# FFN1's first product with the tokens stationary, its gate on token-major tiles, and transposes behind it

## The chip, the cores and the metric

The kernel runs on one core of one Trainium2 chip. The metric is the device time of one execution in microseconds (us); the number given for a kernel is the median of its timed runs. A profiled execution has a trace beside its time: the span runs from the first to the last instruction in it. Engines are called PE (TensorE; PEld is its weight load), DVE (VectorE), ACT (ScalarE), POOL (GpSimd) and SP (the queue that issues most transfers).

## The reference, cut to what matters

256 tokens of width 2048 go through two blocks. The change lies in the feed-forward part of the first one:

```python
D_MODEL, SEQ, D_FF = 2048, 256, 5632

def _rmsnorm(x, g, eps=1e-6):
    return x * lax.rsqrt(jnp.mean(x * x, axis=-1, keepdims=True) + eps) * g

def first_block(x, ...):
    ...                                   # mixer: attention, recurrence, w_out
    x = x + _rmsnorm(mix, g_mix_post)
    h = _rmsnorm(x, g_ffn_pre)            # (256, 2048)
    gu = h @ w_ffn_in                     # (2048, 2 * 5632): gate columns, then up columns
    f = silu(gu[..., :D_FF]) * gu[..., D_FF:]
    x = x + _rmsnorm(f @ w_ffn_out, g_ffn_post)
    return x
```

All values are float32.

## The kernel before, in words

Every large product multiplies in the `fp32r` form, with each operand split into a high and a low part; three of the four products of parts are summed. Weights come in tiles `W` of 512 KB (128 partitions x 1024 floats). For each, `split` (L157 to L163) issues the load on SP, lets ACT write the high part `WH` (L162) and DVE the low part `WL` (L163). There are three buffers each of `WH` and `WL` and four of `W`. The activations lie in `HL` tiles, high and low part side by side. One such weight tile with its products is the unit of this document: FFN1's first product has 176 of them, its second one (`w_ffo`) 88. SP issues the loads in program order.

There are two forms of the product.

- `gemm_t` (L182) keeps the weights stationary: a 128 x 128 piece of `WH` is loaded into PE and the tokens' high and low parts stream past it together (512 columns, L210), then a piece of `WL` with the high part alone (256 columns, L209 or L212). One weight tile is 8 such pairs, 16 matmuls. The result has features on the partitions and tokens along the free axis, with the two halves of the sum next to each other, so that an evacuation has to add them. With `lead=4` the first four tiles are gone through once for each half of the tokens, in matmuls of 256 and 128 columns.
- `gemm_steps` (L107) keeps the tokens stationary: a 128 x 128 piece of `HL` is loaded and 512 columns of `WH` or `WL` stream past it, three matmuls (L145, L146, L147) for each of 2 token halves and 2 slices of depth, 12 matmuls for one weight tile. The result has tokens on the partitions and is already the whole sum. With `lead=4` it goes through the first four tiles for the first token half, then for the second.

`ffn1` (L1131) runs in three parts of 8, 8 and 6 feature blocks of 256. For each block the gate product and the up product are made (4 weight tiles each), and then, for each of the two 128-feature halves of a block, this follows: ACT copies one half of the sum (L1145), DVE adds the other (L1146); for the gate DVE multiplies by `R` (L1152), ACT takes the silu (L1154) and POOL multiplies by `R` again (L1155); for the up part DVE multiplies by the gate (L1161), ACT writes the high part of f (L1163) and POOL the low one (L1164). `R` is 1/rms of the tokens laid along the free axis; `spread` (L1118) makes it with two matmuls once `rms` (L1105) has summed the squares. After each part the second product with `w_ffo` runs in the `gemm_steps` form over that part's features.

Beside FFN1 a table for the second block is made on POOL: `s5_table` (L1565) computes eight groups by doubling (L1586) and sends each to memory from POOL's own queue (L1590). Its tile `R` has two buffers, so a new group's first write (L1578) waits for the transfer of the group before the last. Each of these chores is a Python generator in a lane; a product calls `tick` twice per weight tile, which advances each lane.

Before FFN1, `w_out` ends with the residual sum and norm: `pn_x` (L1072) adds into `xr`, `pn_tr` (L1082) transposes `xr` on PE (L64, 4 transposes of 128 x 128 into one PSUM tile), and ACT (L1100) and DVE (L1101) write the high and low part of each 128-feature slice, scaled by `g_ffn_pre`. `halves_t` (L1409) orders these pieces for `gemm_t`: all four of token half 0 first. `halves` (L1390) orders them for `gemm_steps`. The step from FFN1 to the second block's first product (`w_in_2`, L1195 to L1199) already uses `halves` and `gemm_steps` with a lead.

## Time and profile before

| | before |
|---|---|
| median of 3 runs | 3405.7 us (3399.62 to 3407.25) |
| the profiled execution's own time | 3411.74 us |
| its span | 3409.9 us |
| PE busy | 3291.0 us (97%) |
| PEld busy | 2743.1 us (80%) |
| DVE busy | 2258.8 us (66%) |
| ACT busy | 1697.8 us (50%) |
| POOL busy | 790.3 us (23%) |
| granted PE clock, mean | 0.983 of full speed |
| `w_ffi` loads, issue to landing | 176 of 512 KB, 3.9 us |

The shares are means over the whole span; a stage has its own. A granted clock of 1.00 is 2.4 GHz and one of 0.50 is 1.2 GHz.

### The profile page before, as it was taken

How to read it: one execution, taken by the hardware profiler on the slowest of the kernel's cores; microseconds unless marked ns; L12 is line 12 of the kernel's file. 1: busy time of each engine (PE TensorE's matmuls, PEld its weight loads, DVE VectorE, ACT ScalarE, POOL GpSimd, SP SyncE). 2: the span in 40 equal slices, each digit the busy share in tenths (PEclk: the TensorE clock that was granted, in tenths of full speed). 3: DMA queues.
4: the chain of work that ended last, by engine and by line, in shares of the span. 5: the costliest groups of instructions: out<-in, count | busy, mean ns of one | idle time of the engine just before them, and what ended most of it. 6: DMA issues, size and time to landing. Idle time of an engine off the chain costs nothing.

```text
span 3409.9 us, 50346 instructions
## 1 busy us (share of the span) xinstructions
PE 3291.0 (97%) x18954; PEld 2743.1 (80%) x18954; DVE 2258.8 (66%) x3505; ACT 1697.8 (50%) x2641; POOL 790.3 (23%) x970
## 2 busy tenths in 40 slices
PE   8999999999999999999999999899999999999998
PEld 7887777877888888888888887677677888888886
DVE  5776786855666766654555557966777775666576
ACT  5545455444555445444443444365555554454453
POOL 0203122422111204880210212720121321111021
PEclk9999999999999999999999999999999999999999
DMA  6453543556656774556566566445356456656664
GB/s 214 155 181 101 162 131 123 177 160 210 196 177 210 245 251 145 191 191 194 187 188 193 186 196 227 145 160 191 116 193 200 145 185 192 188 186 192 191 186 154
DMA packets 180485, 615.19 MB, mean 180 GB/s; under 512 B 23099, under 2 KB 28300, under 8 KB 179472
## 3 DMA queue, kind: packets, MB, share of 16 engines
q1 hardware_dynamic: 169088, 580.01, 53.5%
q0 software_dynamic: 10288, 30.33, 2.7%
q8 instruction: 149, 2.44, 0.3%
q10 hardware_dynamic: 864, 1.62, 0.1%
q14 instruction: 96, 0.79, 0.1%
HBM read 588.36 MB, written 26.66 MB: 180 GB/s over the span
## 4 chain that ended last, share of the span: by engine, by line
PE 68%; DVE 8%; issue 8%; POOL 5%; DMA 4%; ACT 2%; DVEq 0%; POOLq 0%; ACTq 0%; SPq 0%
PE pm L210 22%; PE pm L209 10%; PE pm L145 9%; PE pm L146 9%; PE pm L147 9%; DVE WL L163 3%; PE ps L64 1%; POOL s5ro L1586 1%; POOL s5rt L1586 1%; DMA pd<-s5rt 1%; ACT WH L162 1%; DMA T<-dT 1%; PE pm L212 1%; PE ps L1879 0%; DMA dT<-TM 0%
## 5 line engine op out<-in xcount | busy, mean ns | idle before, releaser
L163 DVE TENSOR_TENSOR WL<-W,WH 128x1024 fp32r<-128x1024 f32 (+2 forms) x1016 | 1283.3, 1264 | 828.5 <-ACT WH L162 822.8
L210 PE MATMUL pm<-HL,WH 128*128 128x512 f32 x4928 | 1749.8, 401 | 8.7 <-ACT WH L162 4.4
L162 ACT ACTIVATE WH<-W 128x1024 fp32r<-128x1024 f32 (+2 forms) x1016 | 1066.3, 1050 | 1047.0 <-PE pm L210 442.0
L209 PE MATMUL pm<-HL,WL 128*128 128x256 f32 x4620 | 1315.8, 285 | 17.7 <-DVE WL L163 16.2
L210 PEld LDWEIGHTS pm<-HL,WH 128*128 128x128 f32 x4928 | 916.1, 190 | 213.2 <-DVE pt L495 7.0
L209 PEld LDWEIGHTS pm<-HL,WL 128*128 128x128 f32 x4620 | 878.5, 190 | 42.4 <-DVE WL L163 20.8
L145 PE MATMUL pm<-WH,HL 128*128 128x512 f32 (+1 forms) x1472 | 586.1, 399 | 1.1 <-ACT WH L162 1.1
L146 PE MATMUL pm<-WL,HL 128*128 128x512 f32 (+1 forms) x1472 | 577.8, 393 | 6.7 <-DVE WL L163 6.7
L147 PE MATMUL pm<-WH,HL 128*128 128x512 f32 (+1 forms) x1472 | 575.8, 391 | 0.7 <-DVE HL L1096 0.7
L146 PEld LDWEIGHTS pm<-WL,HL 128*128 128x128 f32 x1472 | 278.1, 189 | 65.3 <-DVE WL L163 9.7
L145 PEld LDWEIGHTS pm<-WH,HL 128*128 128x128 f32 x1472 | 277.5, 189 | 62.2 <-issue 4.1
L147 PEld LDWEIGHTS pm<-WH,HL 128*128 128x128 f32 x1472 | 277.9, 189 | 58.4 <-DVE HL L1096 1.1
L2147 POOL TENSOR_TENSOR fcv<-fcv,fcv 128x256 f32<-128x256 f32 x44 | 51.5, 1170 | 544.6 <-DVE fcv L2134 440.1
L1155 POOL TENSOR_TENSOR sg<-sg,spr 128x256 f32<-128x256 f32 x44 | 43.2, 999 | 303.3 <-ACT sg L1154 303.3
L212 PE MATMUL pm<-HL,WL 128*128 128x256 f32 x308 | 87.3, 283 | 1.4 <-DVE WL L163 1.4
L1164 POOL TENSOR_TENSOR HL<-fu,HL 128x256 fp32r<-128x256 f32 x44 | 49.5, 1143 | 128.5 <-ACT HL L1163 128.5
L2133 DVE SCALAR_TENSOR_TENSOR fcv<-fu,cw,fcv 128x255 f32<-128x255 f32 x88 | 54.3, 617 | 32.4 <-ACT fcv L2132 32.4
L1586 POOL TENSOR_TENSOR s5ro<-s5rt,s5un 128x8 f32<-128x8 f32 (+7 forms) x128 | 73.0, 584 | 4.9
L2132 ACT ACTIVATE fcv<-fu,cw 128x256 f32<-128x256 f32 x88 | 52.5, 596 | 40.5 <-DVE fu L2131 40.5
L212 PEld LDWEIGHTS pm<-HL,WL 128*128 128x128 f32 x308 | 58.6, 190 | 14.8 <-DVE WL L163 2.7
L1145 ACT ACTIVATE fu<-pm 128x256 f32<-128x256 f32 x88 | 33.8, 384 | 64.3 <-PE pm L210 64.3
L1586 POOL TENSOR_TENSOR s5rt<-s5ro,s5ro 128x4 f32<-128x4 f32 (+7 forms) x128 | 64.4, 524 | 4.9
(519 smaller groups left out, 3291.5 us busy)
## 6 DMA issues: line engine op xcount, KB each, us to landing
W<-in_w_ffi SPq DMA_DIRECT2D x176, 512.0 KB, 3.9
W<-in_w_up SPq DMA_DIRECT2D x176, 512.0 KB, 3.6
W<-in_w_rkv SPq DMA_DIRECT2D x96, 512.0 KB, 3.5
W<-in_w_qkv SPq DMA_DIRECT2D x96, 512.0 KB, 3.6
W<-in_w_ffo SPq DMA_DIRECT2D x88, 512.0 KB, 3.9
W<-in_w_down SPq DMA_DIRECT2D x88, 512.0 KB, 3.6
W<-in_w_gate SPq DMA_DIRECT2D x64, 512.0 KB, 3.8
W<-in_w_out SPq DMA_DIRECT2D x64, 512.0 KB, 4.2
```

The lines of the kernel that those rows point to most:

```text
L145: nc.tensor.matmul(o, a, WH[:, j], start=(k == 0), stop=False)
L146: nc.tensor.matmul(o, a, WL[:, j], start=False, stop=False)
L147: self.mm = nc.tensor.matmul(o, b, WH[:, j], start=False, stop=(k == kts - 1))
L162: self.nc.scalar.activation(WH, W, AF.Copy)
L163: self.gated(self.nc.vector.tensor_tensor(WL, W, WH.bitcast(F32), op=ALU.subtract))
L209: nc.tensor.matmul(o[:, 0, ts], WL[:, kk, c], x[:, 0, ts], start=False, stop=False)
L210: self.mm = nc.tensor.matmul(o[:, :, ts], WH[:, kk, c], x[:, :, ts], start=(k == 0), stop=(k == 15))
L212: nc.tensor.matmul(o[:, 0, ts], WL[:, kk, c], x[:, 0, ts], start=False, stop=False)
L1586: i = nc.gpsimd.tensor_tensor(o, x, y, op=op)
L2132: nc.scalar.activation(c, u, AF.Identity, scale=cw[:, 2, ct:ct + 1], bias=cw[:, 3, ct:ct + 1])
L2133: nc.vector.scalar_tensor_tensor(c[:, 1:], u[:, 0:255], cw[:, 1, ct:ct + 1], c[:, 1:], op0=ALU.mult, op1=ALU.add)
L2147: nc.gpsimd.tensor_tensor(c, c, gs[i], op=ALU.mult)
```

## The change

FFN1's first product goes from `gemm_t` to `gemm_steps`, in 11 feature blocks of 512 with 8 weight tiles for the gate and 8 for the up part. The packing of `w_ffi` changes with it; the number and size of the loads stay. The gate is now one ACT instruction for each token half, the silu of the PSUM tile with 1/rms as its scale (in the changed file L1145). The up part is one DVE instruction for each half that multiplies by 1/rms and by the gate (L1149). Then a generator in lane 4, `turn`, transposes the 128 x 512 tile `sg` in four pieces for each half (L64), and ACT and DVE write the high (L1159) and low part (L1160) of f from PSUM. Line numbers behind L1180 fall by 5: the table's lines are L1572 to L1585. The second product is as it was. In front of FFN1 `halves(..., 4)` takes the place of `halves_t`.

```diff
-                self.halves_t(lambda h, q: self.pn_tr(acc, h2[:, :, 0], h2[:, :, 1], "g_ffn_pre", h, q))
+                self.halves(lambda h, q: self.pn_tr(acc, h2[:, :, 0], h2[:, :, 1], "g_ffn_pre", h, q), 4)
...
-            for bi, b in enumerate(range(2 * blocks[0], 2 * blocks[-1] + 2)):
-                gs = []
-
-                def total(P):
-                    u = fp.tile([128, T], F32, tag="fu", bufs=4, name=self.nm("fu"))
-                    nc.scalar.activation(u, P[:, T:], AF.Copy)
-                    nc.vector.tensor_tensor(u, P[:, :T], u, op=ALU.add)
-                    return u
-
-                def ev_g(nb, P):
-                    for i in range(2):
-                        u = total(P[i])
-                        nc.vector.tensor_tensor(u, u, R, op=ALU.mult)
-                        g = fp.tile([128, T], F32, tag="sg", bufs=4, name=self.nm("sg"))
-                        nc.scalar.activation(g, u, AF.Silu)
-                        nc.gpsimd.tensor_tensor(g, g, R, op=ALU.mult)
-                        gs.append(g)
-
-                def ev_u(nb, P):
-                    for i in range(2):
-                        u = total(P[i])
-                        nc.vector.tensor_tensor(u, u, gs[i], op=ALU.mult)
-                        kk = 2 * bi + i
-                        nc.scalar.activation(fH[:, kk], u, AF.Copy)
-                        nc.gpsimd.tensor_tensor(fL[:, kk], u, fH[:, kk].bitcast(F32), op=ALU.subtract)
+            for bi, b in enumerate(blocks):
+                g = fp.tile([128, 2, 512], F32, tag="sg", bufs=2, name=self.nm("sg"))
+
+                def ev_g(nb, P, g=g):
+                    for h in range(2):
+                        nc.scalar.activation(g[:, h], P[h], AF.Silu, scale=r1[:, h:h + 1])
+
+                def ev_u(nb, P, g=g, bi=bi, fH=fH, fL=fL):
+                    for h in range(2):
+                        nc.vector.scalar_tensor_tensor(g[:, h], P[h], r1[:, h:h + 1], g[:, h], op0=ALU.mult, op1=ALU.mult)
+
+                    def turn():
+                        yield 2
+                        for h in range(2):
+                            ps = self.pst()
+                            for u in range(4):
+                                self.T(ps[:, u * 128:u * 128 + 128], g[:, h, u * 128:u * 128 + 128])
+                            pv = ps.rearrange("p (a b) -> p a b", a=4)
+                            hi, lo = (t[:, 4 * bi:4 * bi + 4, h * 128:h * 128 + 128] for t in (fH, fL))
+                            nc.scalar.activation(hi, pv, AF.Copy)
+                            nc.vector.tensor_tensor(lo, pv, hi.bitcast(F32), op=ALU.subtract)
+                            yield
+                    self.spawn(4, turn())
                 if first:
                     P0 = []
-                    for _ in self.gemm_t(self.i["w_ffi"], [b], xa, lambda nb, P: P0.append(P), lead=4, pre=self.pre):
-                        self.tick()
+                    self.gemm(self.i["w_ffi"], [b], NKT, lambda k: xa(k)[:, 0], lambda k: xa(k)[:, 1], lambda nb, P: P0.append(P), lead=4, pre=self.pre)
                     self.drain(0)
                     r1 = self.rms(fp, xr)
                     self.tap("x1", xr)
                 else:
-                    for _ in self.gemm_t(self.i["w_ffi"], [b], xa, ev_g):
-                        self.tick()
-                for n, _ in enumerate(self.gemm_t(self.i["w_ffi"], [22 + b], xa, ev_u)):
+                    self.gemm(self.i["w_ffi"], [b], NKT, lambda k: xa(k)[:, 0], lambda k: xa(k)[:, 1], ev_g)
+                for n, _ in enumerate(self.gemm_steps(self.i["w_ffi"], [11 + b], NKT, lambda k: xa(k)[:, 0], lambda k: xa(k)[:, 1], ev_u)):
                     self.tick()
                     if first and n == 4:
-                        R = self.spread(fp, r1)
                         ev_g(None, P0[0])
                         first = False
...
-    a["w_ffi"], a["w_ffo"] = _pk_t(f["w_ffn_in"][0]), _pk(f["w_ffn_out"][0])
+    a["w_ffi"], a["w_ffo"] = _pk(f["w_ffn_in"][0]), _pk(f["w_ffn_out"][0])
```

Where the instructions stand is read from the built programs. On POOL, in the first part of FFN1, this stands before; `sg` is the gate after the silu, `spr` is `R`, and `s5rt` and `s5ro` are the table's tiles:

```order
L1586 TENSOR_TENSOR s5ro_13019<-s5rt_12987,s5un 128x4x2
L1578 MEMSET s5rt_13245 128x2
L1586 TENSOR_TENSOR s5ro_13018<-s5rt_12987,s5un 128x4x2
...
L1586 TENSOR_TENSOR s5ro_13091<-s5rt_12987,s5un 128x4x8
L1155 TENSOR_TENSOR sg_13050<-sg_13050,spr_12858 128x256
L1155 TENSOR_TENSOR sg_13057<-sg_13057,spr_12858 128x256
L1586 TENSOR_TENSOR s5ro_13090<-s5rt_12987,s5un 128x4x8
```

The same group of the table in the changed program:

```order
L1581 TENSOR_TENSOR s5ro_12878<-s5rt_12848,s5un 128x4x2
L1573 MEMSET s5rt_13065 128x2
L1581 TENSOR_TENSOR s5ro_12877<-s5rt_12848,s5un 128x4x2
...
L1581 TENSOR_TENSOR s5ro_12926<-s5rt_12848,s5un 128x4x8
L1581 TENSOR_TENSOR s5ro_12925<-s5rt_12848,s5un 128x4x8
```

The multiplication of the gate, which stood behind the first write of a new table group, is gone from POOL, and so are the low parts of f (L1164); nothing of FFN1's blocks is left there.

On PE, in the changed program, behind an up product (its last matmul stands right ahead of this) the next gate product begins in `pm_13006` and `pm_13007`, and the transposes of the finished block (`sg_12505`) stand inside it:

```order
L145 MATMUL pm_13006<-WH_13008,HL_12475 128x512
...
L147 MATMUL pm_13007<-WH_13008,HL_12475 128x512
L64 MATMUL ps_13032<-par,sg_12505 128x128 x4
L145 MATMUL pm_13006<-WH_13039,HL_12475 128x512
...
L147 MATMUL pm_13007<-WH_13039,HL_12475 128x512
L64 MATMUL ps_13051<-par,sg_12505 128x128 x4
L145 MATMUL pm_13006<-WH_13039,HL_12475 128x512
```

One whole weight tile (12 matmuls) lies between the last matmul of the block and its first four transposes, half a tile more ahead of the other four. On DVE the two multiplications stand one split later than the last matmul's tile:

```order
L163 TENSOR_TENSOR WL_13040<-W_13041,WH_13039 128x1024
L1149 SCALAR_TENSOR_TENSOR sg_12505<-pm_12803,rr_12781,sg_12505 128x512
L1149 SCALAR_TENSOR_TENSOR sg_12505<-pm_12804,rr_12781,sg_12505 128x512
L163 TENSOR_TENSOR WL_13075<-W_13076,WH_13074 128x1024
L163 TENSOR_TENSOR WL_13099<-W_13100,WH_13098 128x1024
L1160 TENSOR_TENSOR HL_12504<-ps_13032,HL_12504 128x4x128
L1160 TENSOR_TENSOR HL_12504<-ps_13051,HL_12504 128x4x128
```

So they stand ahead of the transposes that read them by the split of one tile, and the low parts of f behind two more.

Where FFN1 begins, PE's rows before are these (`xr` is the residual stream, `HL_12475` its transposed parts, `HL_11820` holds the first four weight tiles, split ahead of time):

```order
L64 MATMUL ps_12476<-par,xr 128x128 x4
L64 MATMUL ps_12489<-par,xr 128x128 x4
L64 MATMUL ps_12524<-par,xr 128x128 x4
L64 MATMUL ps_12560<-par,xr 128x128 x4
L210 MATMUL pm_12505<-HL_12475,HL_11820 128x2x128
L212 MATMUL pm_12505<-HL_12475,HL_11820 128x128
```

and in the changed program:

```order
L64 MATMUL ps_12476<-par,xr 128x128 x4
L64 MATMUL ps_12489<-par,xr 128x128 x4
L145 MATMUL pm_12506<-HL_11820,HL_12475 128x512
...
L64 MATMUL ps_12537<-par,xr 128x128 x4
L146 MATMUL pm_12506<-HL_11820,HL_12475 128x512
L64 MATMUL ps_12550<-par,xr 128x128 x4
L64 MATMUL ps_12579<-par,xr 128x128
L64 MATMUL ps_12593<-par,xr 128x128
```

Two groups of transposes instead of four stand ahead of the first matmul; the next four groups, which read token half 1 too, stand behind the first 16 to 17 matmuls and ahead of the last 7 of token half 0.

## Rows read from the trace of the kernel before

**Rows 1.** The page's first part: busy time, share of the span, instructions

```profile
PE 3291.0 (97%) x18954; PEld 2743.1 (80%) x18954; DVE 2258.8 (66%) x3505; ACT 1697.8 (50%) x2641; POOL 790.3 (23%) x970
```

**Rows 2.** Stages: us; busy us (instructions) of PE, PEld, DVE, ACT, POOL; PEclk; DMA

```profile
1300.77:1326.39 25.62, 23.42 (x161) 21.61 (x161) 22.31 (x74) 17.30 (x54) 9.60 (x26) 0.87 0.24 73
1326.39:1511.12 184.73, 175.08 (x966) 151.15 (x965) 110.08 (x120) 84.03 (x121) 147.94 (x259) 0.97 0.57 186
1511.12:1598.16 87.04, 87.04 (x386) 72.10 (x384) 41.40 (x36) 38.69 (x42) 19.86 (x29) 1.00 0.65 203
1598.16:1778.85 180.69, 180.69 (x1025) 156.95 (x1024) 102.85 (x125) 87.86 (x127) 32.20 (x30) 1.00 0.59 187
...
1865.89:2001.41 135.52, 135.52 (x770) 117.71 (x768) 77.81 (x95) 65.23 (x93) 23.51 (x22) 1.00 0.57 187
```

**Rows 3.** Waits in FFN1's first part: us in total, times, longest us

```profile
DVE fu L1161 <- POOL sg L1155: 20.4, 4, 7.1
...
POOL s5rt L1578 <- DMA pd<-s5rt: 16.7, 6, 4.3
...
PE pm L209 <- DVE WL L163: 9.7, 4, 4.4
```

**Rows 4.** Timeline around one of these stalls: start, us, engine; in brackets idle before

```profile
1433.53 0.10 POOL L1578 MEMSET s5rt<- 128x2 f32 x1 [3.80 <-DMA pd<-s5rt]
...
1435.41 1.40 POOL L1155 TENSOR_TENSOR sg<-sg,spr 128x256 f32<-128x256 f32 x2
1436.17 0.93 DVE L1161 TENSOR_TENSOR fu<-fu,sg 128x256 f32<-128x256 f32 x1 [7.12 <-POOL sg L1155]
...
1437.88 1.31 DVE L163 TENSOR_TENSOR WL<-W,WH 128x1024 fp32r<-128x1024 f32 x1
...
1439.25 0.58 PE L209 MATMUL pm<-HL,WL 128*128 128x256 f32 x1 [4.42 <-DVE WL L163]
```

**Rows 5.** Windows at half clock: in the entry; behind three stalls, first and last

```profile
1309.05:1315.90 6.85, 6.52 (x31) 6.33 (x32) 6.35 (x14) 5.70 (x19) 6.23 (x19) 0.50 0.08 15
1438.80:1442.20 3.40, 2.95 (x10) 2.57 (x11) 2.81 (x3) 1.50 (x2) 3.24 (x4) 0.51 0.56 160
...
1493.40:1496.80 3.40, 3.40 (x12) 2.90 (x11) 1.75 (x2) 0.25 (x1) 3.22 (x6) 0.50 0.90 264
```

**Rows 6.** PE's timeline in the attention: transposes inside a product of the gemm_steps form

```profile
923.38 0.60 PE L64 MATMUL ps<-par,ro 128*128 128x128 f32 x4
923.74 0.48 PE L145 MATMUL pm<-WH,HL 128*128 128x512 f32 x1
...
925.22 0.60 PE L64 MATMUL ps<-par,ro 128*128 128x128 f32 x4
```

**Rows 7.** Timeline of FFN1's entry: PE's first matmul, DVE's last piece of the tokens

```profile
1304.37 0.38 PE L210 MATMUL pm<-HL,HL 128*128 128x256 f32 x1
...
1321.90 0.34 DVE L1101 SCALAR_TENSOR_TENSOR HL<-ps,par,HL 128x128 fp32r<-128x128 f32 x1
```

**Rows 8.** PE's timeline from FFN1's end through w_in_2's block 0 to the next product

```profile
2065.78 0.39 PE L147 MATMUL pm<-HL,HL 128*128 128x512 f32 x1
...
2097.86 0.39 PE L210 MATMUL pm<-HL,WH 128*128 128x512 f32 x1
```

**Rows 9.** Splits: DVE in parts one and two, ACT in part one; busy, mean ns

```profile
L163 DVE TENSOR_TENSOR WL<-W,WH 128x1024 fp32r<-128x1024 f32 x59 | 83.0, 1412 | 51.9 <-ACT WH L162 51.7
...
L163 DVE TENSOR_TENSOR WL<-W,WH 128x1024 fp32r<-128x1024 f32 x64 | 78.4, 1225 | 74.0 <-ACT WH L162 73.5
...
L162 ACT ACTIVATE WH<-W 128x1024 fp32r<-128x1024 f32 x59 | 61.9, 1056 | 58.3 <-PE pm L210 54.0 <-ACT HL L1163 1.7 <-DVE WL L163 1.7
```

**Rows 10.** Operations like the new ones, elsewhere in the kernel: ns min/median/max, forms

```profile
L844 DVE SCALAR_TENSOR_TENSOR m<-pm,r,rope x16: 740/744/752, 753.7 to 991.9; 128x512 f32<-128x512 f32 x16
L1095 ACT ACTIVATE HL<-ps x8: 592/598/602, 2067.3 to 2080.6; 128x512 fp32r<-128x512 f32 x8
L1096 DVE TENSOR_TENSOR HL<-ps,HL x8: 675/680/693, 2068.9 to 2081.2; 128x512 fp32r<-128x512 f32 x8
```

## The prediction

> **What bounds the kernel now.** I read the page first: PE is busy 97% of the span [rows 1], so time is won only where PE's stream gets shorter or where it stands still. Then I cut FFN1 into stages at the first matmul of each [rows 2]: an entry of 25.62 us, in which the first four weight tiles are multiplied while the tokens are still being transposed, and then the two products in turn. The second product (32 tiles, `gemm_steps`) takes 87.04 us, 2.720 us a tile, with PE busy throughout. The first product (`gemm_t`) takes 180.69 us for 64 tiles in the second part and 135.52 us for 48 in the third, 2.823 us a tile, PE busy throughout too. Both forms pass 6,144 columns through PE for a tile, which is 2.560 us at 2.4 GHz; what lies above is 13 ns for each of 12 matmuls in one form and 16 ns for each of 16 in the other. So in these parts PE's own stream is the limit, and the form decides.
>
> The first part is different. Its 60 tiles would take 169.4 us at 2.823; it takes 184.73, with POOL busy 147.94 of them [rows 2]. The waits show why [rows 3]: PE waited 9.7 us in four pieces for DVE's low parts, DVE 20.4 us in four pieces for POOL's gate multiplication, and POOL 16.7 us for the table's transfers to memory. One of the four in the timeline [rows 4]: POOL stands 3.80 us in front of the first write of a new table group, whose buffer is still being sent; the gate is behind it in POOL's queue and starts at 1435.41; DVE, which has nothing else in order, stood 7.12 us; its next split starts at 1437.88 instead of a tile earlier, and PE stands 4.42 us. The clock adds to it: after three of the stalls PE ran 3.40 us each (the first and the last are shown) at 1.2 GHz [rows 5], a loss of half of it, 5.1 us in all. 9.7 and 5.1 account for 14.8 of the 15.3 us.
>
> **Term 1: the parts without stalls.** 112 tiles of parts two and three, now 180.69 + 135.52 = 316.2 us, would be 112 x 2.720 = 304.6 us. The new transposes come on top: 8 for each block of 512 features, in two groups of four. The attention has such groups inside a product of the same form [rows 6]: from 923.38 to 925.22 stand one group and six matmuls; without six times 0.227 the group costs 0.48 us. Its lower bound is the gap to the next matmul's start, 0.36, the upper one the group's own 0.60. I take 0.48, since it has the slow restart of the stream in it. 14 groups are 6.7 us. Gain: 316.2 - 304.6 - 6.7 = 4.9 us (6.6 with 0.36, 3.2 with 0.60).
>
> A rule of the Trainium skill speaks against the new transposes: the page "TensorE: Matmul & The Clock Gate", section "Part 4: PE-mode transpose", puts one of 128 x 128 at about 275 ns in a kernel's context, an estimated 24.2 us for all 88 where the row gives 22 x 0.48 = 10.6, and a forecast 13.6 us higher. The trace disagrees as far as the spacing goes: 0.48 us for four in a running stream [rows 6].
>
> **Term 2: the first part.** From the eighth tile on, 56 tiles are left. Before they take 184.73 - 4 x 2.823 = 173.4 us; after, 56 x 2.720 = 152.3 and 8 groups, 3.8: 156.2 us. Gain 17.3 us. It rests on the stalls' going altogether, and here is why I think so: the gate no longer passes through POOL, nothing of FFN1's blocks stands behind the table's waits, and what is late next is only the table itself, which the second block needs, and FFN1 and its successor's first product last until 2097.86 [rows 8]. The `spread` (two small matmuls, a wait) goes too; I leave it in the 0.5 us.
>
> What could stand in its place are DVE and ACT, which now evacuate PSUM in pieces of 128 x 512. The new operations are not in the trace; the nearest ones take 744 ns (the product with a column and a tile), 598 ns (ACT from PSUM) and 680 ns (the low part) [rows 10]. For 16 tiles DVE has 16 x 1.225 [rows 9] + 2 x 0.744 + 2 x 0.680 = 22.4 us of 44.5, 50%, against 57% in part two before [rows 2]. The tight place is the turn: DVE's two multiplications stand behind the split of the next tile and must be done when PE comes to the transposes, one tile (2.72 us) after the last up matmul. The split's buffer comes free one tile before the end, ACT and DVE need 1.06 and 1.23 to 1.41 us [rows 9], so the split ends before the up product does; the multiplications end about 1.2 to 1.5 us after it. That leaves over 1 us. If this cover were gone, PE would stand, and with it the next gate product. Gate evacuation, high and low parts of f have several tiles of room: nothing. SP's loads are the same in number and size, and POOL's lighter queue only brings the table's transfers forward: nothing.
>
> **Term 3: the entry.** From 1300.77 to the end of the eighth tile it is 25.62 + 4 x 2.823 = 36.9 us before. After, 8 tiles are 21.8 us and the eight groups of transposes of `xr` 3.8, together 25.6, plus what PE waits and loses to the clock. Before, this excess is 25.62 - 11.29 - 3.84 = 10.5 us (the split form of the first four tiles is in it, and 6.85 us at half clock [rows 5]); with that nothing much is won, 0.8 us. The entry to `w_in_2`, which has the form that FFN1 gets, goes from 2065.78 to 2097.86 [rows 8]: 31.85 us for 99 matmuls and eight groups (22.4 + 3.8), an excess of 5.6 us, so a gain of 5.7. A floor for the time: DVE writes the tokens' last piece at 1321.90 [rows 7], two tiles come after it, so not before 1327.7, a gain of at most 10. I take 5.0: near `w_in_2`'s, a little less because ACT and DVE have four scaled pieces to write per group here where they have one there.
>
> **The sum.** 4.9 + 17.3 + 5.0 = 27.2 us off the span of 3409.9: 3382.7. The profiled execution itself took 3411.74, 6.0 above the median of 3405.7; off the median it is **3378.5 us**.
>
> **The rivals.**
>
> *The entry gives nothing or takes.* In the new order four groups of transposes that need token half 1's residual sums stand in PE's queue ahead of the last matmuls of half 0, where PE waits in order; before, PE first had all of half 0 (from 1304.37 [rows 7]). Against it speaks `w_in_2`'s entry. Gain 0 to -5 instead of 5: 3383 to 3388.
>
> *The table holds DVE instead.* POOL no longer pauses for the gate, so its table runs densely beside DVE's splits. In the first part a split took 1412 ns on average and 1225 in the second [rows 9]: POOL's work does slow DVE, but by 0.19 us of a tile's 2.72. If the four stalls and the slow clock came back this way, 14.8 us would be lost: 3393.
>
> *PE's stream gains less.* If a tile's time went by its columns alone, both forms would take the same, and 172 x 0.103 = 17.7 us of the gain would be missing: 3396. For it speaks that both pass 6,144 columns; against it stand the stages themselves, each form at one time per tile to 0.001 us [rows 2]. The page named above comes near this case in its section "Back-to-back issue gap", which gives a warm matmul alone N/2.4 + 2.5 ns, so an estimated 0.010 us a tile between the forms; the stages here show 0.103.
>
> *Slower: the turn is late.* If DVE's multiplications came so late that PE stood at each of the 11 blocks' transposes, it would have to be 34 us in all to be slower by 0.2%, 3.1 us for each block: they would have to end 5.8 us after the up product, not 1.5. It decides from the point at which two splits, not one, stood ahead of them with a late ACT; the order shows one.
>
> *More:* the entry near its floor and shorter groups: 27.2 + 5 + 2.6 is about 35 us, 3371.
>
> **How the numbers follow.** Forecast (3374 to 3382) 0.58; entry gives nothing 0.17; table holds DVE 0.08; stream gains less 0.05; turn late 0.04; more 0.08. The range for 8 in 10 takes in all but the late turn and the far ends: 3370 to 3396. A measurement of this kernel can tell about 0.2%, 6.8 us; faster than 3398.9 are all cases but the late turn and a pile of small losses: 0.93; within it 0.03; slower 0.04.
>
> **What would show it.** In the changed kernel's profile the first product should take 2.72 us a tile and 0.96 more per block: about 178 us for part two and 133.5 for part three, with two groups of transposes per block that wait for nothing. Part one should be within 2 us of part two for as many tiles, no wait of PE for DVE's low parts, no window at half clock between 1340 and 1500, and POOL's part of the table done tens of us earlier. The eighth tile should end about 32 us after `w_out`'s last matmul. It would be wrong if PE waits at the transposes, if the waits for low parts stay, or if the entry's waits and half-clock windows grow.

## The result, and the profile after

The changed kernel takes 3372.15 us (median of 5 runs, 3368.46 to 3375.2), the kernel before 3405.7 beside it (5 runs, 3399.62 to 3409.87): a ratio of 0.9898, with a 95% interval from 0.9885 to 0.9912. The forecast of 3378.5 lies 6.35 us above the result, and the result is inside its range. One of the six runs of e1 below took 3585.07 us, in a slower state with a mean granted clock of 0.845, and is left out of e1's ratio.

The first part of the changed kernel's profile page (before: [rows 1]):

```profile
PE 3264.5 (97%) x18270; PEld 2699.5 (80%) x18270; DVE 2208.5 (66%) x3371; ACT 1667.1 (49%) x2508; POOL 691.0 (21%) x882
```

The stages (us; busy us of PE, PEld, DVE, ACT, POOL; granted clock; DMA), cut as in [rows 2] but for the entry, which here goes to the end of the eighth tile and not of the fourth: entry, part one, `w_ffo`, part two, `w_ffo`, part three, `w_ffo`, then the entry to `w_in_2`.

```profile
1287.64:1317.33 29.69, 27.34 (x130) 21.07 (x130) 28.00 (x74) 21.90 (x58) 22.06 (x46) 1.00 0.30 101
1317.33:1472.49 155.16, 155.16 (x698) 128.51 (x697) 83.74 (x69) 67.51 (x70) 117.01 (x236) 1.00 0.68 216
1472.49:1560.48 87.99, 87.99 (x394) 72.86 (x392) 41.62 (x36) 38.77 (x41) 0.00 (x0) 1.00 0.62 191
1560.48:1737.44 176.96, 176.96 (x794) 146.52 (x792) 86.46 (x77) 76.79 (x80) 0.00 (x0) 1.00 0.61 190
1737.44:1825.47 88.03, 88.03 (x394) 72.86 (x393) 45.43 (x43) 35.04 (x34) 0.00 (x0) 1.00 0.62 192
1825.47:1957.92 132.45, 132.45 (x594) 109.69 (x592) 65.22 (x59) 56.88 (x58) 0.00 (x0) 1.00 0.61 191
1957.92:2023.51 65.59, 65.59 (x294) 54.09 (x292) 43.01 (x55) 32.09 (x42) 0.00 (x0) 1.00 0.67 217
2023.51:2053.83 30.32, 27.06 (x132) 21.86 (x132) 22.59 (x34) 14.48 (x20) 10.54 (x16) 1.00 0.81 280
```

PE is busy in every microsecond of the three parts, and the clock is 1.00 in all of them. Part two is 64 x 2.720 + 6 x 0.48 = 176.96 to the hundredth, part three 48 x 2.720 + 4 x 0.48 = 132.48. The two groups of a part's last block stand in the `w_ffo` behind it, which takes 87.99 and not 87.04. From the end of `w_out` to the end of the last `w_ffo` FFN1 takes 735.87 us; before it was 2066.01 - 1300.77 = 765.24. So 29.4 us are gained in FFN1.

The two spans differ by more, 41.6 us. The rest is not the change's: `w_out` ended at 1300.77 in the one execution and at 1287.64 in the other, with the same instructions ahead of it, and behind FFN1 they took 1343.89 and 1344.79 us. In the 13 traces of this study that have this program ahead of it, it ended between 1287.6 and 1300.8. One profiled span against another therefore tells nothing here below some 13 us. FFN1's own time, from its one end to the other, is steadier: runs that should agree in it do, with 748.84 and 748.85, or 735.87 and 735.83 us (below).

From the waits between 1287 and 1530 us of the changed kernel, POOL's for its transfers and all of PE's (us in total, times, longest):

```profile
POOL s5rt L1573 <- DMA pd<-s5rt: 16.3, 5, 4.9
...
PE pm L147 <- DVE rstd L1066: 1.4, 1, 1.4
PE ps L64 <- DVE xr L1077: 0.8, 2, 0.6
```

POOL still waits 16.3 us for its transfers, about as long as in [rows 3], but nothing of FFN1 stands behind it any more: DVE's wait for POOL (20.4 us) and PE's for low parts (9.7) are gone. The last transfer of the table is issued at 1460.56, where before POOL still computed at 1528.

The turn behind the fourth block (start, us, engine; idle before in brackets):

```profile
1472.20 1.40 DVE L1149 SCALAR_TENSOR_TENSOR sg<-pm,rr,sg 128x512 f32<-128x512 f32 x2
1472.26 0.39 PE L147 MATMUL pm<-WH,HL 128*128 128x512 f32 x1
...
1473.78 1.23 DVE L163 TENSOR_TENSOR WL<-W,WH 128x1024 fp32r<-128x1024 f32 x1 [0.17 <-ACT WH L162]
...
1475.21 0.60 PE L64 MATMUL ps<-par,sg 128*128 128x128 f32 x4
1475.56 0.49 PE L145 MATMUL pm<-WH,HL 128*128 128x512 f32 x1
...
1477.05 0.60 PE L64 MATMUL ps<-par,sg 128*128 128x128 f32 x4
```

The up product's last matmul starts at 1472.26; DVE's two multiplications end at 1473.60, and the transposes come at 1475.21, 1.6 us later, without a wait.

### The profile page after: what moved, and what is told of

The parts are those of the page before. It is cut to its first block, busy times and chain, and to the rows that moved or that the text cites. A ratio compares the mean times of both kernels' runs of the same rounds, so it can differ in the third digit from the quotient of the medians.

```text
span 3368.3 us, 48519 instructions
## 1 busy us (share of the span) xinstructions
PE 3264.5 (97%) x18270; PEld 2699.5 (80%) x18270; DVE 2208.5 (66%) x3371; ACT 1667.1 (49%) x2508; POOL 691.0 (21%) x882
## 4 chain that ended last, share of the span: by engine, by line
PE 73%; DVE 8%; issue 7%; DMA 3%; ACT 2%; POOL 2%; DVEq 0%; POOLq 0%; ACTq 0%; SPq 0%
PE pm L210 15%; PE pm L145 14%; PE pm L146 14%; PE pm L147 14%; PE pm L209 7%; DVE WL L163 3%; PE ps L64 2%; ACT WH L162 1%; DMA T<-dT 1%; PE ps L1874 1%; PE pm L212 0%; PE ps L1829 0%; DMA W<-in_w_br_b 0%; DVE rsz L296 0%; DVE xr L1077 0%
## 5 line engine op out<-in xcount | busy, mean ns | idle before, releaser
L210 PE MATMUL pm<-HL,WH 128*128 128x512 f32 x3552 | 1265.8, 402 | 8.8 <-ACT WH L162 4.1
L209 PE MATMUL pm<-HL,WL 128*128 128x256 f32 x3330 | 950.6, 286 | 6.1 <-DVE WL L163 5.7
L145 PE MATMUL pm<-WH,HL 128*128 128x512 f32 (+1 forms) x2160 | 854.7, 396 | 0.7 <-ACT WH L162 0.7
L146 PE MATMUL pm<-WL,HL 128*128 128x512 f32 (+1 forms) x2160 | 844.6, 391 | 6.5 <-DVE WL L163 6.4
L147 PE MATMUL pm<-WH,HL 128*128 128x512 f32 (+1 forms) x2160 | 843.2, 390 | 0.6 <-DVE HL L1096 0.6
L210 PEld LDWEIGHTS pm<-HL,WH 128*128 128x128 f32 x3552 | 661.0, 190 | 156.6 <-DVE pt L495 6.7
L209 PEld LDWEIGHTS pm<-HL,WL 128*128 128x128 f32 x3330 | 633.1, 190 | 25.9 <-DVE WL L163 8.4
L146 PEld LDWEIGHTS pm<-WL,HL 128*128 128x128 f32 x2160 | 406.5, 188 | 90.7 <-DVE WL L163 9.5
L145 PEld LDWEIGHTS pm<-WH,HL 128*128 128x128 f32 x2160 | 406.2, 188 | 87.9 <-issue 4.5
L147 PEld LDWEIGHTS pm<-WH,HL 128*128 128x128 f32 x2160 | 406.2, 188 | 85.4 <-DVE HL L1096 1.1
L212 PE MATMUL pm<-HL,WL 128*128 128x256 f32 x222 | 63.0, 284 | 1.4 <-DVE WL L163 1.4
L212 PEld LDWEIGHTS pm<-HL,WL 128*128 128x128 f32 x222 | 42.3, 190 | 10.6 <-DVE WL L163 2.2
L2144 POOL TENSOR_TENSOR HL<-fcv,HL 128x256 fp32r<-128x256 f32 x44 | 44.5, 1011 | 23.3 <-ACT HL L2143 23.3
L948 POOL TENSOR_TENSOR gate<-gate,spr 128x256 f32<-128x256 f32 x32 | 26.4, 828 | 93.2 <-DVE gate L947 88.2
```

What stands on the lines that cost most here:

```text
L145: nc.tensor.matmul(o, a, WH[:, j], start=(k == 0), stop=False)
L146: nc.tensor.matmul(o, a, WL[:, j], start=False, stop=False)
L147: self.mm = nc.tensor.matmul(o, b, WH[:, j], start=False, stop=(k == kts - 1))
L209: nc.tensor.matmul(o[:, 0, ts], WL[:, kk, c], x[:, 0, ts], start=False, stop=False)
L210: self.mm = nc.tensor.matmul(o[:, :, ts], WH[:, kk, c], x[:, :, ts], start=(k == 0), stop=(k == 15))
L212: nc.tensor.matmul(o[:, 0, ts], WL[:, kk, c], x[:, 0, ts], start=False, stop=False)
```

## The experiments

FFN1's time in each run is read as above. "Tile" is the time of one weight tile of the first product, inside a part. e10 and e12 were executed once, so they have no interval.

| run | ratio to before (95%) | FFN1, us | tile, us |
|---|---|---|---|
| before | 1 | 765.24 | 2.823 |
| changed | 0.9898 (0.9885 to 0.9912) | 735.87 | 2.720 |
| e1, old form, gate on DVE | 0.9939 (0.9923 to 0.9955) | 748.84 | 2.823 |
| e2, old form, table slower | 0.9936 (0.9921 to 0.9951) | 748.85 | 2.823 |
| e3, new form, old entry | 0.9882 (0.9865 to 0.9899) | 735.21 | 2.720 |
| e6, new form, gate on POOL | 0.9894 (0.988 to 0.9909) | 735.83 | 2.720 |
| e4, transposes twice | 0.9939 (0.9926 to 0.9951) | 744.96 | 2.720 |
| e5, no transposes | 0.9865 (0.9851 to 0.9878) | 725.28 | 2.720 |
| e7, turn at once | 0.99 (0.9885 to 0.9915) | 737.76 | 2.720 |
| e8, cut in two | 0.9937 (0.9925 to 0.995) | 746.47 | 2.783 |
| e9, alternating | 0.9944 (0.9926 to 0.9962) | 747.97 | 2.798, in two levels |
| e10, new operand | one execution: 3386.03 us beside 3410.36 | 746.43 | 2.771, part of it 2.82 |
| e11, halves in turn | 0.9896 (0.988 to 0.9913) | 735.83 | 2.720 |
| e12, old form, transposes | one execution: 3389.69 us beside 3406.77 | 754.89 | 2.77 and 2.82 |

**The stalls.** e1 and e2 keep the old form and take the gate's lateness away in two ways.

```diff
-                        nc.gpsimd.tensor_tensor(g, g, R, op=ALU.mult)
+                        nc.vector.tensor_tensor(g, g, R, op=ALU.mult)
...
-                        nc.gpsimd.tensor_tensor(fL[:, kk], u, fH[:, kk].bitcast(F32), op=ALU.subtract)
+                        nc.vector.tensor_tensor(fL[:, kk], u, fH[:, kk].bitcast(F32), op=ALU.subtract)
```

> The kernel before, with the two pieces of work that FFN1 gives to POOL (the gate's second multiplication by R and the low part of f) put on DVE; form of the product, entry and table as before. Theory (three parts: 15.3 us from the stalls behind POOL's queue and the slow clock after them, 6.7 us from the form less its transposes, 7.2 us from the entry): 3405.7 - 15.3 = 3390 us (3386 to 3395), part one at 169 to 171 us, no wait of PE for DVE's low parts and no window at half clock in part one. Rival 'the form is all': the stalls would only move to another place, 3402 to 3408. Rival 'the stalls are all' (form and transposes cancel, the entry gives nothing): 3372 to 3378.

```diff
-                    yield 2
+                    yield 3
                 nc.gpsimd.dma_start(self.pd[:, ro + 1024 * g:ro + 1024 * g + 1024], R.rearrange("p t k n -> p (t k n)"))
```

> The kernel before, with the table on POOL spread over half as many ticks again (one of its eight steps for every three ticks, not two); nothing else. It leaves the gate on POOL but takes away the table's waits for its own transfers, since each transfer has some 6 us more to land. Theory (the gate is late because it stands in POOL's queue behind a first write that waits for a transfer): these waits fall from 16.7 us to under 4, the stalls go, 3390 us (3386 to 3396). Rival 'POOL is simply too slow beside the gate' (its 80% busy time, not the wait): half of the stalls stay, 3396 to 3402. Rival 'the stalls do not matter': 3405.

The entry, the 60 tiles of part one and part two of e1, cut as in [rows 2] (columns as above):

```profile
1291.50:1315.69 24.19, 20.90 (x162) 18.81 (x161) 23.63 (x65) 17.09 (x54) 16.37 (x34) 1.00 0.24 77
1315.69:1485.44 169.75, 169.75 (x965) 147.58 (x965) 123.26 (x160) 83.60 (x121) 128.12 (x248) 1.00 0.67 208
...
1572.48:1753.18 180.70, 180.70 (x1026) 156.97 (x1024) 112.99 (x155) 87.87 (x127) 0.00 (x0) 1.00 0.62 187
```

Part one is 169.75 us, 60 x 2.823 and 0.36 for the `spread`, where it was 184.73 [rows 2]: 15.0 us of stalls and slow clock, near the 15.3 of the theory. The other 1.4 of the 16.4 us lie in the entry, which e1 does not change: 24.19 us at a clock of 1.00, where [rows 2] have 25.62 at 0.87. It took 24.2 us in e2 and e12 too, which have it unchanged, so those 1.4 us belong to the one traced execution of the kernel before. Part two does not move although DVE has 10 us more to do there. e2's part one comes to the same 169.75 us. But e2 missed its own step: the waits for transfers were to fall under 4 us, and in its part one they read

```profile
POOL sg L1155 <- ACT sg L1154: 26.6, 4, 18.6
...
POOL s5rt L1578 <- DMA pd<-s5rt: 11.2, 4, 4.0
```

They stay at 11.2 us. What changed is the first line. POOL now waits four times for the gate's silu, so its queue is early; in the kernel before it did so once, ahead of the first block:

```profile
POOL sg L1155 <- ACT sg L1154: 18.4, 1, 18.4
```

In e2 the gate starts at most 0.7 us behind its silu, in the kernel before up to 15.4 us (the silu ends at 1419.97, the gate starts at 1435.41 [rows 4]). The wait for a transfer is not harmful as such; what hurt was a queue that ran behind.

**A gate on POOL in the new form.**

```diff
                         nc.scalar.activation(g[:, h], P[h], AF.Silu, scale=r1[:, h:h + 1])
+                        nc.gpsimd.tensor_scalar(g[:, h], g[:, h], r1[:, h:h + 1], None, op0=ALU.mult)
...
-                        nc.vector.scalar_tensor_tensor(g[:, h], P[h], r1[:, h:h + 1], g[:, h], op0=ALU.mult, op1=ALU.mult)
+                        nc.vector.tensor_tensor(g[:, h], P[h], g[:, h], op=ALU.mult)
```

> The changed kernel with a multiplication put back on POOL: after the silu POOL multiplies the gate by 1/rms, and DVE multiplies the up part by the gate alone. So the gate stands behind the table's waits again, in the new form. Theory (a late gate costs only what it is later than the up product: before, one such multiplication began 15.5 us after its silu, at 1435.41, with 11 us of room; here the up product gives 20 us): waits of DVE for POOL under 3 us in all, 3370 to 3376 us. Rival 'any work of FFN1 in POOL's queue brings the stalls back': three or four of 4 to 7 us, with half clock behind them, 3380 to 3388.

The third block in its timeline: silu, POOL's second multiplication, DVE's product with the up part.

```profile
1415.17 1.37 ACT L1145 ACTIVATE sg<-pm,rr 128x512 f32<-128x512 f32 x2 [0.98 <-PE pm L147]
...
1421.18 1.56 POOL L1146 TENSOR_SCALAR sg<-sg,rr 128x512 f32<-128x512 f32 x1
...
1437.12 1.28 DVE L1150 TENSOR_TENSOR sg<-pm,sg 128x512 f32<-128x512 f32 x2
```

POOL is done at 1422.74, 14 us before DVE needs the gate. No wait of DVE for POOL is left, POOL waits 16.2 us for transfers as ever, and FFN1 takes 735.83 us, the changed kernel's time. So the new form is rid of the stalls with the gate's multiplication on POOL too. That the longer up product does it, with 20 us of room, is not shown: the low parts of f, 49.5 us of POOL's time in FFN1 before, are off POOL here as well, and the gate was done at most 8.9 us behind its silu (fourth block), which the 10 to 11 us of room in the old form would have held.

**The entry.**

```diff
-                self.halves(lambda h, q: self.pn_tr(acc, h2[:, :, 0], h2[:, :, 1], "g_ffn_pre", h, q), 4)
+                self.halves_t(lambda h, q: self.pn_tr(acc, h2[:, :, 0], h2[:, :, 1], "g_ffn_pre", h, q))
```

> The changed kernel with the old order of the transposes of the residual stream in front of FFN1 (all four groups of token half 0 first, as for the old form); the form of all products as changed. Theory (of the entry's 7.2 us most comes from the order, which lets PE begin after two groups and not four): 3372.2 + 5 = 3377 us (3374 to 3380), the entry at 33 to 36 us with waits of PE for the residual sums before its first matmul. Rival 'the form of the first tiles brings it' (whole 512-column matmuls in place of pieces of 256 and 128 columns): 3371 to 3374 and an entry of 29 to 31 us.

The theory fell: with the old order FFN1 takes 735.21 us, 0.66 less than the changed kernel. PE's first matmul starts 1.47 us behind `w_out` in both and its second one later, at 3.56 and not 1.80, but its waits up to the eighth tile come to the same, 2.0 us against 2.2. So the order of the transposes is worth nothing, and what is left of the entry's change is the form of the first tiles. e1's entry, in the old order and with the clock at 1.00, takes 24.19 + 4 x 2.823 + 0.36 (the `spread`) = 35.84 us to the end of the eighth tile. e3's takes 29.0 (its first block's transposes start at 1350.37 and `w_out` ended at 1296.85; in the changed kernel the eighth tile ends 24.48 us before those transposes). In e1 the first four tiles go in pairs of 256 and 128 columns, 0.23 us a pair (1306.04 to 1307.88 are eight), so 64 pairs take 14.7 us where four whole tiles take 10.9. That is 3.8 of the 6.8 us. Another 1.2 are waits (3.2 us in e1, 2.0 in e3), 0.4 the next four tiles at 2.823 and not 2.720, 0.36 the `spread`; I can't place the last 1.0.

**The transposes.**

```diff
-                            for u in range(4):
+                            for u in (0, 1, 2, 3, 0, 1, 2, 3):
```

> The changed kernel with each group of four transposes of the finished block made twice into the same PSUM tile, one group right behind the other: 88 transposes more, nothing else. Theory (a group costs 0.48 us in a running stream, of which 0.36 us until the next matmul can start and 0.12 us the slow restart; the second group has no restart of its own): 22 x 0.36 = 7.9 us more in FFN1, which is 744 us then and not 735.9. Rival (each transpose takes the 272 ns of its row, one after the other): 88 x 0.272 = 23.9 us more. Rival (only the interruption costs, further transposes are nearly free): under 3 us more.

```diff
-                            ps = self.pst()
-                            for u in range(4):
-                                self.T(ps[:, u * 128:u * 128 + 128], g[:, h, u * 128:u * 128 + 128])
-                            pv = ps.rearrange("p (a b) -> p a b", a=4)
+                            pv = g[:, h].rearrange("p (a b) -> p a b", a=4)
```

> The changed kernel without the transposes of the finished blocks: ACT and DVE write the high and the low part of f from the SBUF tile as it stands, so f is not transposed and what is computed is another thing; all other work is as in the changed kernel. Theory (22 groups at 0.48 us, no other wait hangs on them): FFN1 at 735.9 - 10.6 = 725.3 us, the kernel 10.6 us below the changed one. Rival by 88 x 0.272: 23.9 us below. Rival (they stand in gaps that would be there anyway): no difference over 3 us.

Without them FFN1 is 735.87 - 725.28 = 10.59 us shorter, and 22 x 0.48 is 10.56. The second group right behind a first one costs (744.96 - 735.87) / 22 = 0.413 us, a little over the 0.36 that I expected. One group of eight in e4:

```profile
1437.06 1.03 PE L64 MATMUL ps<-par,sg 128*128 128x128 f32 x8
1437.85 0.48 PE L145 MATMUL pm<-WH,HL 128*128 128x512 f32 x1
1438.17 0.40 PE L146 MATMUL pm<-WL,HL 128*128 128x512 f32 x1
```

0.79 us to the next matmul where four take 0.35, and the restart (0.32 to the second matmul, not 0.227) is there once. Each of these transposes has a duration of 272 ns in its row, so a price per row, 24 us for 88, is refuted.

**The turn's cover.**

```diff
                     def turn():
-                        yield 2
                         for h in range(2):
```

> The changed kernel without the pause of one weight tile ahead of the transposes: the first four stand right behind the block's last up matmul. Theory (in the changed kernel DVE's two multiplications end 0.4 and 1.1 us after that matmul, so the pause is the cover): PE waits 0.5 to 1.1 us at each of 11 blocks, 5 to 12 us in all, FFN1 at 741 to 748 us, and perhaps half clock behind some of the waits. Rival (the cover is not needed, since PE's queue runs ahead by that much): FFN1 at 736 to 738 us.

FFN1 takes 737.76 us, 1.9 more, which is the rival's range and not the theory's. Of the 1.9, 0.7 are not the turn's: in this execution PE ran at half clock in the entry, ahead of the first turn,

```profile
1295.59:1299.01 3.42, 3.42 (x9) 2.57 (x9) 3.42 (x9) 2.40 (x6) 1.49 (x4) 0.50 0.05 17
```

and the eighth tile ended 30.39 us behind `w_out` and not 29.69. From one block's transposes to the next ones are 44.59 us where the changed kernel has 44.47, so the turn costs 0.12 us a block. In the built program two matmuls still stand between the up product and the transposes, and the trace shows what is left of the wait:

```profile
1431.75 0.39 PE L146 MATMUL pm<-WL,HL 128*128 128x512 f32 x1
1432.04 0.66 PE L64 MATMUL ps<-par,sg 128*128 128x128 f32 x4
1432.45 0.48 PE L147 MATMUL pm<-WH,HL 128*128 128x512 f32 x1
```

0.29 and 0.41 us where the stream has 0.227 and 0.35. DVE starts on the first half of the block before the last matmul of the second half is through, so only the first multiplication is waited for. The pause of a whole tile is more cover than is needed.

**Where the form's 0.103 us a tile come from.** The old form has 16 matmuls a tile, half of them of 256 columns; the new one 12 of 512. e8 cuts the middle one of three in the new form.

```diff
-                nc.tensor.matmul(o, a, WL[:, j], start=False, stop=False)
+                for c in range(0, cols, cols // cut):
+                    nc.tensor.matmul(o[:, c:c + cols // cut], a, WL[:, j, c:c + cols // cut], start=False, stop=False)
```

> The changed kernel with the middle one of each three matmuls in FFN1's first product (the one with the weights' low part, L146) cut into two of 256 columns with the same stationary tokens: 16 matmuls a tile, 8 of 512 and 8 of 256 columns, as in the old form, with the same 6,144 columns; 168 tiles, the first block's gate product not. Theory (a tile's time goes by the number and the width of its matmuls, not by which operand stays): 2.82 us a tile, FFN1 at 735.9 + 17.3 = 753 us. Rival (13.3 ns for each matmul, as in the new form): 2.773 us a tile, 9.0 us more. Rival (the operand that stays decides, a cut costs nothing): 2.72 us a tile and no difference.

A tile took 2.783 us: 0.063 of the 0.103, between the two theories. e9 puts the two pieces apart, so that narrow and wide alternate (`low` multiplies by `WL` over a range of columns, from a start and so many wide).

```diff
+                if cut and k:
+                    low(0, 256)
                 nc.tensor.matmul(o, a, WH[:, j], start=(k == 0), stop=False)
...
+                elif k:
+                    low(256, 256)
```

> As the run with the middle matmul cut in two, but with the two pieces of 256 columns not side by side: one stands ahead of the first matmul of 512 columns, one behind it (the first slice of depth of a product keeps them side by side), so that wide and narrow matmuls alternate as in the old form; the same 6,144 columns a tile. With the pieces side by side a tile took 2.783 us, 0.063 more than uncut and 0.041 less than the old form. Theory (a narrow matmul alone between wide ones is what costs the old form the rest): 2.82 us a tile, FFN1 at about 752 us. Rival (the rest is that the weights stay and the tokens stream): 2.783 us a tile, FFN1 at 746.5 us.

2.798 us on the mean of a block, between the theories again, and the mean hides the point. Here are four starts; the first and second are eight narrow-wide pairs apart, the third and fourth too:

```profile
1405.10 0.28 PE L145 MATMUL pm<-WL,HL 128*128 128x256 f32 x1
...
1407.88 0.28 PE L145 MATMUL pm<-WL,HL 128*128 128x256 f32 x1
...
1432.44 0.28 PE L145 MATMUL pm<-WL,HL 128*128 128x256 f32 x1
...
1435.28 0.28 PE L145 MATMUL pm<-WL,HL 128*128 128x256 f32 x1
```

The first eight take 2.78 us, the other eight 2.84, with the clock at 1.00 and no wait. Averaged over longer stretches, the stream has two levels: 13.3 ns above the columns for each matmul, or 16.5. Where it changes from one to the other, that is at the start of a product or at transposes. Two more runs tried a cause in the neighbours: a matmul that shares its stationary piece or its PSUM tile with the one before.

> As the alternating run (which took 2.798 us a tile, 0.025 less than the old form), but ordered so that no two matmuls next to each other have the same stationary piece of the tokens: narrow and wide ones alternate between the two token halves and the high and low parts, the same 16 matmuls and 6,144 columns a tile (the first slice of depth as in the changed kernel). In the runs before, three of four neighbours kept the same piece; in the old form none do. Theory (a matmul whose stationary piece differs from its neighbour's costs the rest): 2.82 us a tile, FFN1 at 751 to 753 us. Rival (the operand's role or something else of the old form costs it): 2.798 us a tile, FFN1 at 748 us.

> The changed kernel with another order of the six matmuls of each slice of depth in all products of its form (some 560 weight tiles in the whole kernel, leads and tails as before): the two token halves in turn, so that no two neighbours have the same stationary piece of the tokens and none accumulates into the same PSUM tile. What the two runs with a cut and alternating matmuls differ in was this: 2.798 us a tile where 12 of 16 neighbours shared the piece and the PSUM tile, 2.771 where none shared the piece and few the PSUM tile, 2 to 4 ns for each such neighbour. Theory (sharing costs that much in the uncut form too, where 4 of 12 share the piece and 8 of 12 the PSUM tile): 2.69 to 2.71 us a tile, FFN1 at 729 to 733 us, the kernel 5 to 16 us below the changed one. Rival (13 ns for each matmul, whoever its neighbour is; the difference of the two runs comes from the cut pieces alone): 2.72 us a tile, no difference.

Their edit writes the matmuls of one slice of depth in another order (`a` and `b` are the tokens' high and low parts, the number is the token half):

```diff
+                    for n, i, s in (("L", 0, a), (0, 1, a), ("R", 0, a), (0, 0, b), ("L", 1, a), (0, 0, a), ("R", 1, a), (0, 1, b)):
...
+                    for n, (i, s, w_) in enumerate(((0, a, WH), (1, a, WL), (0, b, WH), (1, a, WH), (0, a, WL), (1, b, WH))):
```

Both refute it. e10 stood at 13.3 ns in most of its stretches and at 16.5 in the first block of all three parts, up to its first transposes (from one block's transposes to the next ones inside a part 45.30 us, 2.771 a tile; FFN1 746.4 us). e11 has 2.720 us a tile and a time that can't be told from the changed kernel's. So the last run puts transposes into the old form, once behind the first tile of each gate product.

```diff
+                        if n == 1:
+                            ps = self.pst()
+                            for u in range(4):
+                                self.T(ps[:, u * 128:u * 128 + 128], xr[:, 0, u * 128:u * 128 + 128])
```

> The kernel before with the gate's work on DVE as in the first run here, and one group of four transposes (of the residual stream, read by nobody) behind the first weight tile of each gate product after the first. In the two alternating runs the time above the columns was not one number: it stood at 13.3 ns for each matmul in some stretches and at 16.5 in others, and changed at transposes or at a product's start; the old form, which has no transposes in it, stands at 16.5 throughout. Theory (a group of transposes takes the stream to the lower level, whatever the form): behind each group the old form runs at 16 x 13.3 ns above its columns, 2.77 us a tile instead of 2.823, until the up product or the next gate product begins. Rival (the higher level belongs to the old form): 2.823 us a tile as before, and each of the 21 groups costs 0.36 to 0.48 us more.

Behind a group (at 1354.38), and behind the start of the up product (its first narrow matmul at 1363.38), again eight pairs each:

```profile
1355.52 0.28 PE L209 MATMUL pm<-HL,WL 128*128 128x256 f32 x1
...
1358.30 0.28 PE L209 MATMUL pm<-HL,WL 128*128 128x256 f32 x1
...
1365.60 0.28 PE L209 MATMUL pm<-HL,WL 128*128 128x256 f32 x1
...
1368.43 0.28 PE L209 MATMUL pm<-HL,WL 128*128 128x256 f32 x1
```

2.78 us and 2.83. Behind each of the 21 groups the transposes take the old form to the lower level, and the next product's start takes it back. From one group to the next are 22.87 us, where eight tiles of the old form are 22.58: 0.29 for a group that cost 0.48 in the new form, so some 0.19 is won back. So the old form's 0.103 us are two things: four more matmuls at 13.3 ns, 0.053, and 16 matmuls at 16.5 and not 13.3, 0.051. Why a product's start sets the higher level is open. In the old form and in e9 its first slice of depth has two narrow matmuls side by side, but that is neither enough nor needed. In e9 the first up product of part two begins with such pairs (the first at 1594.95) and stays at the lower level; in e10 no product does, and its first gate product of part two goes to the upper one. Eight pairs each:

```profile
1594.95 0.40 PE L145 MATMUL pm<-WL,HL 128*128 128x256 f32 x2
...
1596.81 0.28 PE L145 MATMUL pm<-WL,HL 128*128 128x256 f32 x1
...
1599.58 0.28 PE L145 MATMUL pm<-WL,HL 128*128 128x256 f32 x1
```

```profile
1574.56 0.28 PE L150 MATMUL pm<-WL,HL 128*128 128x256 f32 x1
...
1575.26 0.28 PE L150 MATMUL pm<-WL,HL 128*128 128x256 f32 x1
...
1578.09 0.28 PE L150 MATMUL pm<-WL,HL 128*128 128x256 f32 x1
```

They take 2.77 us in e9 and 2.83 in e10.

## Why the prediction was right, point by point

- **What bounds the kernel.** Right: PE's stream and PE's stalls in part one, nothing else. DVE and ACT at half load had room throughout.
- **Term 1.** Predicted a gain of 4.9 us; 316.2 - (176.96 + 132.45 + 4 x 0.48) = 4.9. The weighed rule (the Trainium skill, "TensorE: Matmul & The Clock Gate", section "Part 4: PE-mode transpose") puts about 275 ns on one transpose of 128 x 128 in a kernel's context, measured there in bf16. The trace agrees as to the row's duration, 272 ns; as a price in a running stream e5 gives 0.12 us each.
- **Term 2.** Predicted 17.3; 173.4 - (155.16 + 2 x 0.48) = 17.3, of which e1 shows 15.0 as stalls and clock, and the rest, 2.3, is the form and the `spread` less the transposes. The reason was right but not the only one: I let the stalls go because the gate leaves POOL. By e6 they would have gone with it still there, once the low parts were off. The turn's cover was there as worked out (1.1 us from the up product's end to the end of the multiplications; I had 1.2 to 1.5), and by e7 losing most of it costs 0.12 us a block.
- **Term 3** was mis-sized: 5.0 predicted, 36.9 - 29.7 = 7.2 measured, the eighth tile at 29.7 us and not 32. The step that failed is the excess that I gave the new entry, 5.6 us from `w_in_2`'s entry and 0.7 more for the scaled pieces. The new entry's excess is 29.7 - 25.6 = 4.1 us. `w_in_2`'s was the right measure, but the row that I took it from ran partly at half clock:

```profile
2066.01:2097.86 31.85, 28.77 (x132) 23.38 (x132) 22.67 (x34) 14.53 (x20) 10.56 (x16) 0.95 0.77 266
```

In the changed kernel's trace the same entry takes 30.32 us at 1.00, an excess of 4.1 as well. So 1.5 of the missing 2.2 us are that half clock, and 0.7 the allowance for the scaled pieces, which cost nothing. Nor does all of the 7.2 belong to the change: 1.4 are what the 6.85 us at half clock cost in the old entry of the one trace before, and against e1's entry at full clock 5.8 are left. That this is near the 5.0 is luck, since the two half clocks about cancel in the forecast. By e1 against e3 the narrow pieces of the old lead are the largest part. The rival "the entry gives nothing", which went by the order of the transposes, looked at the wrong thing: e3 shows that the order is neutral.
- **The sum.** 4.9 + 17.3 + 7.2 = 29.4 us, against 27.2. Off 3405.7 that is a ratio of 0.9914, just outside the measured interval; the medians differ by 33.6. The entry to `w_in_2` is 1.5 us shorter in the changed kernel's trace, but it runs at 1.00 in e1 too, and all that follows FFN1 takes 0.9 us longer, so nothing is gained there. In each of the eleven kernels of the table with an interval the ratio gives more than FFN1's gain, by 0.5 to 10 us. FFN1's 765.24 us is from the only trace of the kernel before, and where the rest lies is open.
- **The other rivals.** The table beside DVE's splits: in part one a split took 75.86 us / 56 = 1355 ns, against 1412 before, and PE waited for none. PE's stream gaining less: refuted by 2.720 us a tile. The other rule (the Trainium skill, the same page, section "Back-to-back issue gap") gives 2.5 ns above the columns for a warm matmul alone; it is not the price in FFN1's streams, which stand at 13.3 ns at best.

## What to carry to other kernels

Count the matmuls, not only the columns: here each costs 13 ns above its columns, so the form that moves the same columns in fewer and wider ones wins. Transposing the result, 0.48 us for four, is paid for here because the gate and the up product share one result: 16 tiles gain 1.65 us and the eight transposes take 0.96, while a product of 8 tiles by itself would gain 0.82. A late helper engine costs only what it is later than its reader: before you move work off it, see how far its queue runs behind and how long the reader's own work takes, since another engine (e1) and a thinner chore (e2) cured these stalls equally. And measure a change by the time between two events around it in the trace, when the time ahead of it scatters by more than the effect; read the granted clock of every row that you take as a measure, since half clock came and went between executions of the same code (FFN1's entry before and in e1, `w_in_2`'s entry before and after).

## What was not expected of the hardware

A PE stream of alternating wide and narrow matmuls has two speeds at the same clock, 13.3 and 16.5 ns above the columns per matmul, for tens of us on end. Four transposes switch it to the faster one, and the start of a product in the old form to the slower one (e12); in e9 and e10 some products' starts leave the level as it is. FFN1's streams of 512-column matmuls alone stood at 13.3 ns throughout.
